# Attention with a bias on one core: a planner's new settings (grouped outputs, 17 listed VectorE slots, throttled first loads, later copies of V)

## The chip, the cores and the metric

The kernel runs on one core of a Trainium2 chip. The metric is the device time of one execution in microseconds, the median of several runs. Lower is better.

## The reference

For 4 x 8 heads of 1024 rows and 64 columns, in float32:

```python
scores = q @ k.transpose(0, 1, 3, 2) / np.sqrt(64) + bias        # bias: 1024 x 1024, the same for all heads
scores_max = np.max(scores, axis=-1, keepdims=True)
attn = np.exp(scores - scores_max) / (np.sum(np.exp(scores - scores_max), axis=-1, keepdims=True) + 1e-8)
out = attn @ v
```

## The kernel before

**Slots.** A head's 1024 query rows are cut into 8 chunks of 128. One chunk of one head is a *slot*; there are 256. The 32 heads form 16 pairs, the pairs two groups of 7 and 9 (`GROUPS`). A slot needs the 128 x 1024 scores (transposed, keys on partitions) in PSUM, their exponential in bfloat16 in SBUF, and the product with V.

**Three places.** PSUM holds three score tiles, `places[0..2]` (the profile calls them `pl`). Place x takes only slots with first index x. Bias is not added for each head: it is written once into a place by a matmul (L241, 8 matmuls), and each later slot of the same chunk adds to what stands there the new head's scores minus the old head's (`fill`, L244, 8 matmuls of 128 columns; the operands `ko`, `qo` and the negated copies `ke`, `qe` of two heads are stacked for that). 17 slots start a chunk and need the bias matmuls: 0 to 2, 42 to 44, 56, 70 to 72, 166 to 168, 186 and 202 to 204. A place can be filled anew only after its reader has finished.

**Exponentials.** ScalarE takes most slots with one ACTIVATE (`exp`, L258, 128 x 1024) into one of `NE` = 13 tiles `E`. Some slots of place 2 go to VectorE instead, in six steps (`d_steps`): `dy` (L275) reads the place and frees it, then `df`, `dt`, `df`, `dt`, `de` (L280 to L295) work in SBUF. The place is free after `dy`; the rest may be spread out.

**Outputs.** `av` (L312) multiplies a slot's E tile with V: 8 matmuls of 65 columns, V's 65th column being ones, so that the row sum comes along. Seven or six outputs share a PSUM bank `po`; `evac` then divides on VectorE (`rs` L320, `ob` L322) and the stores go out by SP's queue, the last ones by ScalarE's. A bank with a single output uses the one tile `olast`; `ob` has two buffers.

**Loads.** GpSimd's queue loads q, k, v and bias and casts them to bfloat16 (L138 to L165). Raw q and k are transposed by TensorE into `px` (L187, L191), copied out by VectorE (`ko` L199, `qo` L201), and doubled or negated (L210 to L218) or moved by SP's queue (L538). V is copied on VectorE from its landing tile (two buffers) into a ring `vall` (L492). The first pass is the 28 loads that carry pairs 0 to 6 and all bias; pairs 7 to 15 (`EARLY` = 7 onward) follow. For these later loads `issue` puts a one-element GpSimd copy into `tick` (L467) ahead of a load, which waits until the load two before has landed (`LATE` = 2). The first pass has no such wait; its loads wait only for free buffers.

**The order is planned while the program is built.** Each engine's queue is in order. A loop at the end of the kernel keeps a clock for each engine (`t_pe`, `t_act`, `t_dve`, `t_pool`), estimated costs (`FILL`, `AV`, `EXP`, ...) and landing times (`raw_at`, `vland_at`, `bias_at`), and always emits the step that could start first by these clocks. `pe_cands` offers TensorE fills, output matmuls and transposes, `pe_pick` chooses; `dve_pick` chooses for VectorE among copies, evacuations and the steps of VectorE slots. A slot goes to VectorE if `may_d` allows it and the estimated VectorE backlog is below `ROOM`. `DUE` gives the slot by which a later pair's transposes shall be done. Where a clock is wrong, the order stays as planned and the engine waits on the chip.

In this order TensorE's outputs are planned slot by slot, because `round_of` has one value for each slot:

```python
group = [s for s in avq[:1] if round_of[s] == round_of[avq[0]]]
```

Of the kernel before, what the change touches and what calls it, by code (L numbers as in the profile page):

```python
# [16 lines left out]
def kernel(  # L17
# [33 lines left out]
    NE = 13  # L51
# [37 lines left out]
    slots = []  # L89
    round_of = []  # L90
    first_pair, split_pair, group_of = set(), set(), {}
    pr0 = 0
    for g, n in enumerate(GROUPS):
        heads = list(range(2 * pr0, 2 * (pr0 + n)))
        rounds = []
        a = (len(heads) * 2 // 3 + 1) // 2 * 2
        tail = [(2, c, h, h == heads[a]) for c in (3, 4) for h in heads[a:]]
        assert len(tail) <= a
        middle = [[(0, 3, h, h == heads[0]), (1, 4, h, h == heads[0])] + tail[i:i + 1] for i, h in enumerate(heads[:a])]
        ends = [[[(x, c + x, h, h == heads[0] and (go or g == 0)) for x in range(3)] for h in heads]  # L100
                for go, c in enumerate((5, 0) if g % 2 else (0, 5))]
        rounds = ends[0] + middle + ends[1]
        first_pair.add(pr0)
        group_of[pr0] = g
        split_pair.add(heads[a] // 2)
        for r in rounds:
            round_of += [len(slots)] * len(r)
            slots += r
        pr0 += n
# [13 lines left out]


    dslots = set()
    may_d = [x[0] == 2 and 36 < s < NS - 18 and not any(y[3] for y in slots[s:s + 4]) for s, x in enumerate(slots)]

# [207 lines left out]
    with tc.manual_schedule():  # L335
# [15 lines left out]
        nc.gpsimd.memset(qs[D:, :, :], 0.0)  # L351
        for c in (1, 2):
            load_b(c)
        load_k(1)
        load_q(1, slice(0, C0))
        load_v(0)
        load_k(2)
        load_q(2, slice(0, NCH))
        for i in range(10):
# [33 lines left out]

        FILL, BIAS, AV = 452, 500, 264
        L_PE, L_ACT, L_DVE = 205, 210, 140
# [3 lines left out]
        bias_at = {0: T0, 1: T0, 2: 9600}  # L399
        raw_at = {(1, 1, 0): 10800, (1, 0, 0): 11500, (2, 1, 0): 14300, (2, 0, 0): 16000}  # L400
        v_at, vland_at = {}, {0: 13000}
        t_dma = 15900
        DUE = (64, 82, 94, 106, 117, 126, 134, 142, 150)
        t_pe, t_act, t_dve, t_pool = 9300.0, 9900.0, 9600.0, 9000
# [27 lines left out]
        TR, SWITCH = 56, 190  # L432
        LATE, QCOST = 2, 4400
        flight = []
        LAG, AVG = 7, 247
# [4 lines left out]
        ROOM = 5000  # L440
        MARGIN = 0
        WINDOW = 4
# [13 lines left out]
        def freed(pr, t):  # L456

            free_lands.add(pr)
            while loads and loads[0] - LANDS in free_lands:
                load(loads.pop(0), t)  # L460

        def issue(at, cost, depth, load, pr, *a):

            nonlocal t_dma
            if 0 < depth <= len(flight):
                what, t = flight[-depth]
                nc.gpsimd.tensor_copy(tick[:], what)  # L467
                at = max(at, t + 100)
            at = pool(at, 750)
            t_dma = max(t_dma + cost, at + 2200 + cost)  # L470
            flight.append((load(pr, *a), t_dma + 200))
            return t_dma + 200
# [17 lines left out]
        def move_v(pr):  # L490
            def run(t2):
                nc.vector.tensor_copy(vall[:, 2 * pr % VR:2 * pr % VR + 2, :, :D], lands[pr, "v"][:])  # L492
                v_at[pr] = t2 + 480 + L_DVE
                next_v(v_at[pr])
            dve_q.append((vland_at[pr], 0.3, 480, run))


        def early(kind, pr):
            if kind == "k":
                raw_at[pr, 1, 0] = issue(0, 1600, 0, load_k, pr) + SLACK  # L500
            elif kind == "q":
                cs = slice(0 if pr >= SPLIT else C0, NCH)
                raw_at[pr, 0, cs.start] = issue(0, 1600 if pr >= SPLIT else 1100, 0, load_q, pr, cs) + SLACK
            elif kind == "v":
                vland_at[pr] = issue(0, 1600, 0, load_v, pr)
                move_v(pr)
            else:
                bias_at[pr] = issue(0, 1600, 0, load_b, pr)

# [65 lines left out]
        def pe_cands():  # L575

            out = []
            for x in range(3):
# [4 lines left out]
                if r is not None and (before[s] is None or before[s] in used):  # L583
                    cost = FILL + BIAS * bool(slots[s][3] and s > 1)

                    def do(t, s=s, x=x, cost=cost):
# [4 lines left out]
                        next_fill = min([y[0] for y in queue.values() if y], default=NS)  # L591
                        if may_d[s] and backlog(t) < ROOM and len(open_d) < 3:
                            dslots.add(s)
# [7 lines left out]
            todo = []  # L601
            if avq:
                group = [s for s in avq[:1] if round_of[s] == round_of[avq[0]]]
                have = [s for s in group if s in e_at]
                lag = len([s for s in avq[:NE] if s in e_at])
                if len(have) < len(group):
                    group = have if lag >= LAG and have[:1] == avq[:1] else []
                if avq[0] >= NS - 3:
                    group = [s for s in avq[:1] if s in e_at]
                if group and all(slots[s][2] // 2 in v_at for s in group):  # L610
                    todo.append((max(max(e_at[s], v_at[slots[s][2] // 2]) for s in group), group))
            if dav:
                todo.append((dav[0][0], [dav[0][1]]))
            if todo:
                r, group = min(todo)
                b = len(closed)
                if b_tag:
                    tag = b_tag[0]
                    group = group[:7 - len(bank[b][1])]
# [3 lines left out]
                cost = AVG * len(group) if len(group) > 1 else AV  # L623
                if r < 1e11:
                    def do(t, group=group, b=b, tag=tag, cost=cost):
# [10 lines left out]
                        n = len(bank[b][1])  # L636
                        if n == 7 or n == 6 and not (dav and dav[0][0] < t + cost + 600) or len(av_done) in (NS - 1, NS):
                            closed.append(b)
                            b_tag.clear()
                            close(b, tag, t + cost + L_PE)  # L640
                    out.append((max(t_pe, r), cost, do, 1, 0))
            if pieces:
# [4 lines left out]
                if ((pr, which, c0) in raw_at and next_fill >= need - AHEAD and (ring < 0 or last_slot[ring] < next_fill)  # L647
                        and (lag < 4 or need - next_fill < 8)):
# [3 lines left out]
                    urgent = need - next_fill < 12  # L652
                    if r < 1e11:
                        def do(t, pr=pr, which=which, c0=c0, n=n, tag=tag, cost=cost):
# [15 lines left out]
                            dve_q.append((t + cost + L_PE, 0 if urgent else 2, 60 * n + (180 if which else 300), run))  # L670
                        out.append((max(t_pe, r), cost, do, 2 if next_fill < need - 9 else 0.5, 0))
            return out
# [19 lines left out]
        chains, d_wait, open_d = [], [], set()  # L692

        def backlog(t):
            x = max(0, t_dve - t) + sum(y[2] for y in dve_q if y[0] < t + 3000 and y[1] < 3)
            return x + sum(sum(y[0] for y in c) for c in chains) / 2 + sum(sum(y[0] for y in c[1:]) for r, s, c in d_wait) / 2

# [32 lines left out]
        def pe_pick():  # L730
# [5 lines left out]
            if others and NE <= next_act < len(acts) and acts[next_act - NE] not in av_done:  # L736

                return min(others, key=lambda x: (x[3] != 1, x[0]))
            now = [x for x in fills if x[0] <= t_pe]
            if now:  # L740


                short = len([s for s in avq[:NE] if s in e_at]) > NE - 3
                due = [x for x in others if x[3] in ((0.5, 1) if short else (0.5,)) and x[0] <= t_pe]
                if due and act_free() - FILL - L_PE - MARGIN > t_pe + due[0][1]:
# [10 lines left out]
        def dve_pick():  # L756
            can = [x for x in dve_q if x[1] < 4 or len(dav) < 2]
            if not can:
# [4 lines left out]
            if best[1] >= 3:  # L763
                soon = [x for x in dve_q if x[1] < 3 and x[0] < start + 350]
                if soon:
# [3 lines left out]
        move_v(0)  # L769
        for x in ("k3", "q3", "v1", "k4", "q4", "v2", "k5", "q5", "v3", "k6", "q6", "v4", "v5", "b3", "q0", "q1", "b4", "v6", "b5", "b6", "b7"):  # L770
            early(x[0], int(x[1]))
        while next_fill < NS or next_act < len(acts) or avq or dav or dve_q or sp_q:
            c = []
            if next_act < len(acts):
# [21 lines left out]
            if who == 0:  # L796
# [3 lines left out]
                next_act += 1  # L800
                used[s] = e_at[s] = t_act + L_ACT
            elif who == 1:
                dve_q.remove(d)
# [39 lines left out]
```

## Time and profile before

| | |
|---|---|
| median of 3 runs | 233.25 us (232.87 to 233.69) |
| the profiled execution | 235.16 us, span 233.4 us from its first to its last instruction |
| granted TensorE clock, mean | 0.997 |
| ACTIVATE rows of exponentials | 237 (235 whole, 2 halves of slot 0) |
| VectorE slots | 20 |
| matmuls and transposes | 4671 rows |
| DMA | 29.75 MB, mean 127 GB/s |

The profile gives each engine's busy time, a timeline with starts and lengths, the waits (who waited for whom), the chain of work that ended last, and the DMA issues with their time to landing. Rows of ScalarE and TensorE overlap their neighbours, so the distance between starts, not the length of a row, is an instruction's cost in a full stretch. In the timeline, neighbouring rows of the same kind are merged, with a count behind "x", and the idle time before a row stands in brackets with what ended it.

### The profile page before, as it was taken

To read this page: it belongs to the slowest core of one execution; us is meant where nothing else is said; L and a number is where in the kernel's file an instruction comes from. 1 tells how busy PE (TensorE), PEld (TensorE's weight loads), DVE (VectorE), ACT (ScalarE), POOL (GpSimd) and SP (SyncE) were. 2 spreads that over 40 slices of the span, in tenths; PEclk is the share of its full clock that TensorE was granted. 3 is DMA by queue.
4 is the path that set the end of the run, shared out by engine and by line. 5 is a ranking of instruction groups with operands and counts; after the bars stand their busy time and mean duration, and the time that the engine had idled before them with its cause. 6 is when DMAs were issued, how large, how long until landed. Compare 5 with 4: busy or idle time off the path is not lost. (4 is left out here: it accounts for less than half of the span.)

```text
span 233.4 us, 10703 instructions
## 1 busy us (share of the span) xinstructions
PE 222.3 (95%) x4671; PEld 209.3 (90%) x4671; DVE 201.5 (86%) x296; ACT 221.1 (95%) x241; POOL 63.4 (27%) x99
## 2 busy tenths in 40 slices
PE   7989999899999999999999997999999999999992
PEld 2869999798999999999999997999999999999982
DVE  2576677599999998999999869999998999999972
ACT  3799999988999999999999998999999999999993
POOL 8943135055446555245352310000000000000000
PEclk9999999999999999999999999999999999999998
DMA  6999979959999899999999992111111111221212
GB/s 206 206 205 215 224 166 158 229 121 150 120 191 137 131 159 183 204 196 157 197 163 201 204 194 68 44 42 39 44 37 42 45 42 42 65 59 42 66 48 56
DMA packets 55646, 29.75 MB, mean 127 GB/s; under 512 B 31472, under 2 KB 51952, under 8 KB 55600
## 3 DMA queue, kind: packets, MB, share of 16 engines
q0 software_dynamic: 30336, 14.06, 48.7%
q1 hardware_dynamic: 24832, 14.40, 22.6%
q8 instruction: 36, 0.59, 1.1%
q10 hardware_dynamic: 432, 0.62, 0.8%
q14 instruction: 10, 0.08, 0.1%
HBM read 29.36 MB, written 8.39 MB: 162 GB/s over the span
## 5 line engine op out<-in xcount | busy, mean ns | idle before, releaser
L258 ACT ACTIVATE E<-pl 128x1024 bf16<-128x1024 f32 (+1 forms) x237 | 218.0, 1089 | 4.3 <-PE pl L244 3.9
L312 PE MATMUL po<-vall,E 128*128 128x65 bf16 x1888 | 93.6, 194 | 0.9 <-ACT E L258 0.9
L312 PEld LDWEIGHTS <-E 128*128 128x128 bf16 x1888 | 78.1, 98 | 1.9 <-ACT E L258 1.2
L244 PE MATMUL pl<-qo,ko 128*128 128x128 bf16 x1024 | 77.3, 219 | 1.7 <-DVE dy L275 1.1
L244 PEld LDWEIGHTS <-ko 128*128 128x128 bf16 x1160 | 69.2, 98 | 4.5 <-issue 1.5
L244 PE MATMUL pl<-qe,ke 128*128 128x128 bf16 x888 | 66.8, 219 | 1.9 <-DVE qe L212 0.5
L244 PEld LDWEIGHTS <-ke 128*128 128x128 bf16 x888 | 53.2, 98 | 5.0 <-issue 1.3
L275 DVE TENSOR_SCALAR dy<-pl 128x1024 int32<-128x1024 f32 x20 | 24.4, 1220 | 2.1 <-PE pl L244 1.4
L322 DVE TENSOR_TENSOR ob<-po,rs 128x448 f32<-128x448 f32 (+2 forms) x39 | 23.2, 594 | 1.9 <-DVE rs L320 0.5
L295 DVE SCALAR_TENSOR_TENSOR de<-dy,dt 128x1024 uint16<-128x1024 int32 x20 | 24.4, 1218 | 0.0
L290 DVE SCALAR_TENSOR_TENSOR dt<-df,dt 128x1024 f32<-128x1024 f32 x20 | 24.4, 1218 | 0.0
L284 DVE SCALAR_TENSOR_TENSOR dt<-df 128x1024 f32<-128x1024 f32 x20 | 24.3, 1217 | 0.0
L287 DVE SCALAR_TENSOR_TENSOR df<-dt,df 128x1024 f32<-128x1024 f32 x20 | 24.3, 1216 | 0.0
L199 DVE COPY ko<-px 128x1024 bf16<-128x1024 bf16 (+1 forms) x16 | 10.7, 671 | 6.9 <-PE px L191 6.3
L165 POOL DMA_DIRECT2D v<-in_v_dram x16 | 11.4, 712 | 18.3 <-DVE vall L492 16.0
L138 POOL DMA_DIRECT2D q<-in_q_dram x18 | 16.0, 890 | 1.3 <-DMA out_dram<-ob 0.5
L201 DVE TENSOR_SCALAR qo<-px,sgn 128x1024 bf16<-128x1024 bf16 (+2 forms) x18 | 12.4, 688 | 4.4 <-PE px L191 3.6
L280 DVE TENSOR_SCALAR df<-dy 128x1024 f32<-128x1024 uint16 x20 | 13.8, 690 | 0.0
L241 PE MATMUL pl<-ident,braw 128*128 128x128 bf16 x136 | 11.5, 228 | 0.1
L145 POOL DMA_DIRECT2D k<-in_k_dram x15 | 11.0, 734 | 2.2 <-PE pl L244 1.0
L320 DVE RECIPROCAL rs<-po 128x7 f32<-128x7 f32 (+3 forms) x40 | 7.8, 195 | 4.4 <-PE po L312 4.0
L467 POOL COPY tick<-q 1x1 bf16<-1x1 bf16 x9 | 3.8, 421 | 24.7 <-DMA q<-in_q_dram 24.7
(54 smaller groups left out, 129.5 us busy)
## 6 DMA issues: line engine op xcount, KB each, us to landing
v<-in_v_dram POOLq DMA_DIRECT2D x16, 256.0 KB, 6.1
k<-in_k_dram POOLq DMA_DIRECT2D x15, 256.0 KB, 5.6
out_dram<-ob SPq DMA_DIRECT2D x32, 96.0 KB, 3.6
out_dram<-ob SPq DMA_DIRECT2D x45, 64.0 KB, 3.2
ke<-ko SPq DMA_DIRECT2D x22, 128.0 KB, 4.9
q<-in_q_dram POOLq DMA_DIRECT2D x18, 128.0 KB, 4.8
qe<-q SPq DMA_DIRECT2D x17, 128.0 KB, 4.9
out_dram<-ob SPq DMA_DIRECT2D x67, 32.0 KB, 1.8
```

The costliest lines, as they stand in the source:

```text
L138: nc.gpsimd.dma_start(out=t[:, :, y, :], in_=(qf, kf)[x][pr][:, y].rearrange("p (c d) -> p c d", d=D))
L201: nc.vector.tensor_scalar(t["qo"][:, cs, :], px[:], sgn[:], None, op0=ALU.mult)
L244: nc.tensor.matmul(to, kk[:, kc, :], qq[:, c, :], start=False, stop=True, skip_group_check=True)
L258: nc.scalar.activation(e[:, i:i + n].rearrange("p b x -> p (b x)"), places[slots[s][0]][:, i:i + n].rearrange("p b x -> p (b x)"), ACTF.Ex ...
L275: w.tensor_scalar(t["y"][:], places[slots[s][0]].rearrange("p b x -> p (b x)"), scale * LOG2E * 65536.0, 127.0 * 65536.0, op0=ALU.mult, op ...
L280: w.tensor_scalar(t["f"][:], t["lo"], G / 65536.0, None, op0=ALU.mult)
L284: w.scalar_tensor_tensor(t["t"][:], t["f"][:], -G, t["f"][:], op0=ALU.add, op1=ALU.mult)
L287: w.scalar_tensor_tensor(t["f"][:], t["t"][:], Q, t["f"][:], op0=ALU.mult, op1=ALU.add)
L290: w.scalar_tensor_tensor(t["t"][:], t["f"][:], V, t["t"][:], op0=ALU.add, op1=ALU.mult)
L295: w.scalar_tensor_tensor(etile[s].bitcast(U16).rearrange("p c q -> p (c q)"), t["y"][:], 1.0 / 512.0, t["t"][:], op0=ALU.mult, op1=ALU.add)
L312: nc.tensor.matmul(po[:, j + i, :], etile[s][:, kc, :], vall[:, slots[s][2] % VR, kc, :], start=j + i + kc == 0, stop=kc == NCH - 1, skip_ ...
L322: nc.vector.tensor_tensor(ob[:, :n, :], po[:, :n, :D], rs[:, :n, :].to_broadcast([P, n, D]), op=ALU.mult)
```

## The change

- **Outputs in groups.** `pe_cands` may offer one, two or three output products together, if they follow each other in the queue and belong to the same head; `av` then interleaves their matmuls over the eight blocks of keys. A group is offered if its last exponential is planned to be ready within `WAIT`; its planned costs are 264, 504 and 741 ns. Larger groups rank ahead of smaller ones, and outputs of VectorE slots ahead of both.
- **VectorE slots from a list.** `PLAN` names 17 slots; `may_d`, `ROOM` and `backlog` go.
- **First loads three in flight.** The 21 loads after the first seven are no longer emitted ahead of the loop, but in it, each behind a copy into `tick` that waits for the load three before (`FIRST` = 3). Their order changes a little: v5 and v6 come later, behind b3, the rest of q0 and q1, and b4. Loads of pairs 7 to 15 start when this list is empty. The planned time of a tick copy, 180 ns, is now counted, and a load's planned DMA time is 1420 instead of 1600 ns.
- **Copies of V placed later.** For pairs from 7 on the planner places the copy 2500 ns after the landing that it expects.
- **Margins.** `DUE`, `MARGIN` (0 to 50), the planned landings of the first loads, and several thresholds of `pe_pick`, `pe_cands` and `dve_pick`.

The diff, cut to its core:

```diff
-    may_d = [x[0] == 2 and 36 < s < NS - 18 and not any(y[3] for y in slots[s:s + 4]) for s, x in enumerate(slots)]
+    PLAN = (50, 59, 62, 87, 93, 123, 132, 147, 162, 171, 180, 192, 195, 210, 216, 231, 246)
...
+        flight = [(load_b(1), 7700), (load_b(2), 9000), (load_k(1), 10400), (load_q(1, slice(0, C0)), 11000),
+                  (load_v(0), 12400), (load_k(2), 13800), (load_q(2, slice(0, NCH)), 15800)]
...
-        FILL, BIAS, AV = 452, 500, 264
+        FILL, BIAS, AV = 452, 500, (0, 264, 504, 741)
...
-        DUE = (64, 82, 94, 106, 117, 126, 134, 142, 150)
+        DUE = (34, 108, 102, 116, 123, 136, 128, 98, 110)
...
-            while loads and loads[0] - LANDS in free_lands:
+            while loads and not early_loads and loads[0] - LANDS in free_lands:
...
                 nc.gpsimd.tensor_copy(tick[:], what)
-                at = max(at, t + 100)
+                at = pool(max(at, t + 100), 180)
...
-            dve_q.append((vland_at[pr], 0.3, 480, run))
+            dve_q.append((vland_at[pr] + 2500 * (pr >= EARLY), 0.3, 480, run))
+        def early_at():
+            kind, pr = early_loads[0][0], int(early_loads[0][1])
+            if kind == "v" and pr > 1 and pr - 2 not in v_at or kind in "kq" and pr > LANDS and pr - LANDS not in free_lands:
+                return None
+            return max(t_pool, flight[-FIRST][1] + 100)
...
-                raw_at[pr, 1, 0] = issue(0, 1600, 0, load_k, pr) + SLACK
+                raw_at[pr, 1, 0] = issue(0, 1420, FIRST, load_k, pr) + SLACK
...
-                        if may_d[s] and backlog(t) < ROOM and len(open_d) < 3:
+                        if s in PLAN and len(open_d) < 3:
...
+            for n in range(1, 3 + 1):
+                group = avq[:n]
+                if len(group) < n or group[-1] not in e_at or slots[group[0]][2] // 2 not in v_at or n > 1 and (
+                        slots[group[-1]][2] != slots[group[0]][2] or group[-1] >= NS - 3):
+                    break
+                r = max(v_at[slots[group[0]][2] // 2], *[e_at[s] for s in group])
+                if n == 1 or r <= max(t_pe, todo[0][0]) + WAIT:
+                    todo.append((r, AV[n], group))
...
-                        if n == 7 or n == 6 and not (dav and dav[0][0] < t + cost + 600) or len(av_done) in (NS - 1, NS):
+                        if n == 7 or n == 6 and not (dav and dav[0][0] < t + cost + 2000) or len(av_done) in (NS - 1, NS):
...
-                short = len([s for s in avq[:NE] if s in e_at]) > NE - 3
-                due = [x for x in others if x[3] in ((0.5, 1) if short else (0.5,)) and x[0] <= t_pe]
+                short = len([s for s in avq[:NE] if s in e_at]) > NE - 2
+                due = [x for x in others if x[3] < (1.1 if short else 0.6) and x[0] <= t_pe]
...
-                soon = [x for x in dve_q if x[1] < 3 and x[0] < start + 350]
+                soon = [x for x in dve_q if x[1] < 3 and x[0] < start + 600]
...
-        for x in ("k3", "q3", "v1", "k4", "q4", "v2", "k5", "q5", "v3", "k6", "q6", "v4", "v5", "b3", "q0", "q1", "b4", "v6", "b5", "b6", "b7"):
-            early(x[0], int(x[1]))
+        early_loads = ["k3", "q3", "v1", "k4", "q4", "v2", "k5", "q5", "v3", "k6", "q6", "v4", "b3", "q0", "q1", "b4", "v5", "b5", "v6", "b6", "b7"]
...
+            if early_loads and early_at() is not None:
+                c.append((early_at(), 4))
```

More of the change, by code (lines that the diff above doesn't have):

```diff
@@ L106 @@
         for r in rounds:
-            round_of += [len(slots)] * len(r)
             slots += r
@@ L351 @@
         nc.gpsimd.memset(qs[D:, :, :], 0.0)
[L352 to L358, printed above, removed]
+        flight = [(load_b(1), 7700), (load_b(2), 9000), (load_k(1), 10400), (load_q(1, slice(0, C0)), 11000),
+                  (load_v(0), 12400), (load_k(2), 13800), (load_q(2, slice(0, NCH)), 15800)]
         for i in range(10):
@@ L399 @@
         bias_at = {0: T0, 1: T0, 2: 9600}
-        raw_at = {(1, 1, 0): 10800, (1, 0, 0): 11500, (2, 1, 0): 14300, (2, 0, 0): 16000}
+        raw_at = {(1, 1, 0): 10500, (1, 0, 0): 11100, (2, 1, 0): 14000, (2, 0, 0): 16200}
         v_at, vland_at = {}, {0: 13000}
-        t_dma = 15900
-        DUE = (64, 82, 94, 106, 117, 126, 134, 142, 150)
+        t_dma = 15200
+        DUE = (34, 108, 102, 116, 123, 136, 128, 98, 110)
         t_pe, t_act, t_dve, t_pool = 9300.0, 9900.0, 9600.0, 9000
@@ L432 @@
         TR, SWITCH = 56, 190
-        LATE, QCOST = 2, 4400
-        flight = []
-        LAG, AVG = 7, 247
+        FIRST, LATE, QCOST = 3, 2, 4400
+        WAIT = 200
         free_lands, loads, loads_v = set(), list(range(EARLY, NP)), []
@@ L439 @@
         DEP = 115
-        ROOM = 5000
-        MARGIN = 0
+        MARGIN = 50
         WINDOW = 4
@@ L456, in freed @@
         def freed(pr, t):
-            free_lands.add(pr)
-            while loads and loads[0] - LANDS in free_lands:
+            free_lands.update([pr] * (pr is not None))
+            while loads and not early_loads and loads[0] - LANDS in free_lands:
                 load(loads.pop(0), t)
@@ L494, in run @@
                 next_v(v_at[pr])
-            dve_q.append((vland_at[pr], 0.3, 480, run))
+            dve_q.append((vland_at[pr] + 2500 * (pr >= EARLY), 0.3, 480, run))
[4 more added lines that the diff above has]
+            return max(t_pool, flight[-FIRST][1] + 100)
         def early(kind, pr):
             if kind == "k":
-                raw_at[pr, 1, 0] = issue(0, 1600, 0, load_k, pr) + SLACK
+                raw_at[pr, 1, 0] = issue(0, 1420, FIRST, load_k, pr) + SLACK
             elif kind == "q":
                 cs = slice(0 if pr >= SPLIT else C0, NCH)
-                raw_at[pr, 0, cs.start] = issue(0, 1600 if pr >= SPLIT else 1100, 0, load_q, pr, cs) + SLACK
+                raw_at[pr, 0, cs.start] = issue(0, 1420 if pr >= SPLIT else 1000, FIRST, load_q, pr, cs) + SLACK
             elif kind == "v":
-                vland_at[pr] = issue(0, 1600, 0, load_v, pr)
+                vland_at[pr] = issue(0, 1420, FIRST, load_v, pr)
                 move_v(pr)
             else:
-                bias_at[pr] = issue(0, 1600, 0, load_b, pr)
+                bias_at[pr] = issue(0, 1420, FIRST, load_b, pr)
         def doubles(pr, which, c0, n, t2, urgent):
@@ L601, in pe_cands @@
             todo = []
[L602 to L611, printed above, removed]
+            for n in range(1, 3 + 1):
[6 more added lines that the diff above has]
+                    todo.append((r, AV[n], group))
             if dav:
-                todo.append((dav[0][0], [dav[0][1]]))
-            if todo:
-                r, group = min(todo)
+                todo.append((dav[0][0], AV[1], [dav[0][1]]))
+            for r, cost, group in todo:
                 b = len(closed)
@@ L618, in pe_cands @@
                     tag = b_tag[0]
-                    group = group[:7 - len(bank[b][1])]
+                    if len(group) + len(bank[b][1]) > 7:
+                        continue
                 else:
@@ L622, in pe_cands @@
                     r = max(r, f)
-                cost = AVG * len(group) if len(group) > 1 else AV
                 if r < 1e11:
@@ L640, in do @@
                             close(b, tag, t + cost + L_PE)
-                    out.append((max(t_pe, r), cost, do, 1, 0))
+                    out.append((max(t_pe, r), cost, do, 0.75 if group[0] in dslots else 1.1 - 0.1 * len(group), 0))
             if pieces:
@@ L647, in pe_cands @@
                 if ((pr, which, c0) in raw_at and next_fill >= need - AHEAD and (ring < 0 or last_slot[ring] < next_fill)
-                        and (lag < 4 or need - next_fill < 8)):
+                        and (lag < 7 or need - next_fill < 6)):
                     f, tag = min((x_free[y], y) for y in x_free)
@@ L651, in pe_cands @@
                     cost = n * TR + SWITCH * (pr < EARLY or which not in BESIDE)
-                    urgent = need - next_fill < 12
+                    urgent = need - next_fill < 16
                     if r < 1e11:
@@ L670, in do @@
                             dve_q.append((t + cost + L_PE, 0 if urgent else 2, 60 * n + (180 if which else 300), run))
-                        out.append((max(t_pe, r), cost, do, 2 if next_fill < need - 9 else 0.5, 0))
+                        out.append((max(t_pe, r), cost, do, 2 if next_fill < need - 7 else 0.5, 0))
             return out
@@ L692 @@
         chains, d_wait, open_d = [], [], set()
-        def backlog(t):
-            x = max(0, t_dve - t) + sum(y[2] for y in dve_q if y[0] < t + 3000 and y[1] < 3)
-            return x + sum(sum(y[0] for y in c) for c in chains) / 2 + sum(sum(y[0] for y in c[1:]) for r, s, c in d_wait) / 2
         def start_d(s):
@@ L736, in pe_pick @@
             if others and NE <= next_act < len(acts) and acts[next_act - NE] not in av_done:
-                return min(others, key=lambda x: (x[3] != 1, x[0]))
+                return min(others, key=lambda x: (not 0.7 < x[3] < 1.1, x[0]))
             now = [x for x in fills if x[0] <= t_pe]
             if now:
-                short = len([s for s in avq[:NE] if s in e_at]) > NE - 3
-                due = [x for x in others if x[3] in ((0.5, 1) if short else (0.5,)) and x[0] <= t_pe]
+                short = len([s for s in avq[:NE] if s in e_at]) > NE - 2
+                due = [x for x in others if x[3] < (1.1 if short else 0.6) and x[0] <= t_pe]
                 if due and act_free() - FILL - L_PE - MARGIN > t_pe + due[0][1]:
@@ L756, in dve_pick @@
         def dve_pick():
-            can = [x for x in dve_q if x[1] < 4 or len(dav) < 2]
+            can = [x for x in dve_q if x[1] < 4 or len(dav) < 3]
             if not can:
@@ L801 @@
                 used[s] = e_at[s] = t_act + L_ACT
+            elif who == 4:
+                x = early_loads.pop(0)
+                early(x[0], int(x[1]))
+                freed(None, t)
             elif who == 1:
```

1 line of the change is left out of this document (removed).

## The prediction

> **What bounds the kernel now.** I read the busy times of the page, then ScalarE's timeline, then the waits and the timelines around its gaps, last the loads and the end. A gain or loss below 0.3% (0.7 us) I count as no change; a measurement of this kernel cannot tell less.
>
> From the page:
>
> ```profile
> PE 222.3 (95%) x4671; PEld 209.3 (90%) x4671; DVE 201.5 (86%) x296; ACT 221.1 (95%) x241; POOL 63.4 (27%) x99
> ```
>
> TensorE and ScalarE look equally full, so I ask which of them sets the pace. ScalarE's timeline (start, length, rows merged; idle before):
>
> ```profile
> 9.05 7.93 ACT L258 ACTIVATE E<-pl 128x512 bf16<-128x512 f32 x9 [0.47 <-PE pl L244]
> 17.19 30.08 ACT L258 ACTIVATE E<-pl 128x1024 bf16<-128x1024 f32 x32 [0.21 <-PE pl L244]
> ...
> 55.28 17.52 ACT L258 ACTIVATE E<-pl 128x1024 bf16<-128x1024 f32 x19 [0.59 <-PE pl L244]
> 73.14 69.23 ACT L258 ACTIVATE E<-pl 128x1024 bf16<-128x1024 f32 x75 [0.34 <-PE pl L244]
> 143.24 86.31 ACT L258 ACTIVATE E<-pl 128x1024 bf16<-128x1024 f32 x94 [0.87 <-PE pl L244]
> ```
>
> and two rows of narrower views, a stretch near the end and the last exponential:
>
> ```profile
> 217.40 11.23 ACT L258 ACTIVATE E<-pl 128x1024 bf16<-128x1024 f32 x12
> 228.25 1.31 ACT E L258
> ```
>
> From 217.40 to the last start at 228.25 lie 12 steps: 0.904 us each, though a single row lasts longer (1.02 us alone; rows overlap). That is ScalarE's own pace. Against it: 143.24 to 228.25 holds 93 steps, 85.01 - 93 x 0.904 = 0.94 us lost. 55.28 to 143.24 holds 94: 2.98 lost. 17.19 to 55.28 holds 39 (32 and seven in rows left out here): 2.83 lost. 9.05 to 17.19 (a half of 0.495, eight whole): 0.41 lost. So ScalarE sets the end; all it can win is these 7.16 us, and each exponential more costs 0.904. TensorE has room: a slot is 445 ns of scores and 260 of output matmuls (starts in its timeline), 705 against 904; it costs only where it is late.
>
> Where the 7.16 lies, by starts of exponentials: 1.03 at 46.26 to 50.00, where TensorE does this:
>
> ```profile
> 46.30 0.69 PE L241 MATMUL pl<-ident,braw 128*128 128x128 bf16 x8
> 46.82 0.61 PE L244 MATMUL pl<-qz,ko 128*128 128x128 bf16 x8
> 47.27 0.42 PE L312 MATMUL po<-vall,E 128*128 128x65 bf16 x8
> 47.53 0.69 PE L241 MATMUL pl<-ident,braw 128*128 128x128 bf16 x8
> ```
>
> bias, scores, outputs: 47.53 - 46.30 = 1.23 us per slot, three times. The same at 71.6 (bias slots 70 to 72, after four output groups in a row): 0.65. At 141.3 another 1.03, whose cause stands in VectorE's timeline:
>
> ```profile
> 138.33 0.43 DVE L492 COPY vall<-v 128x1024 bf16<-128x1024 bf16 x1 [1.86 <-DMA v<-in_v_dram]
> 138.68 1.22 DVE L295 SCALAR_TENSOR_TENSOR de<-dy,dt 128x1024 uint16<-128x1024 int32 x1
> 139.81 0.74 DVE L201 TENSOR_SCALAR qo<-px,sgn 128x1024 bf16<-128x1024 bf16 x1
> ...
> 141.32 1.22 DVE L275 TENSOR_SCALAR dy<-pl 128x1024 int32<-128x1024 f32 x1
> ```
>
> A copy of V, placed too early, blocks VectorE 1.86 us for its load; the step that frees place 2 (dy) starts late, and the waits name it: TensorE waits 1.1 us for dy, ScalarE then 0.9. Further: 0.39 at 15.9 and 0.54 at 42 to 44 (transposes wait in TensorE's queue for the loads of q2 and of the rest of q0), 0.25 at 38.2 (a transpose), 0.74 at 53.6 (VectorE slots 47 and 50, dy late). The remaining 2.53 are 20 VectorE slots at about 0.1 each (the last stretch: nine of them, 0.94) and 0.31 and 0.29 at 110.6 and 120.9, a VectorE slot beside a transpose.
>
> **The change, part by part.** *17 VectorE slots instead of 20.* The orders of both programs show 17 dy instructions against 20. Three exponentials return to ScalarE: +3 x 0.904 = **+2.71 us** on the path. VectorE is relieved of 3 x (5 x 1.22 + 0.69) = 20.4 us, beside the path; it goes from 86% to about 77%, so fewer dy come late. The new slots lie 3 to 36 apart; 59 and 62, 192 and 195 still follow each other on place 2. With an exponential as 0.904, 0.24 from its end to the fill, 0.445 fill and 0.26 to the next exponential (rows around 43 and 49.7 us), two remaining places turn in 0.945, so some 0.1 per slot stays. I leave the whole 2.53 in, lower bound 1.36 (17 at 0.08, no collisions), upper 5 (all 17 at 0.3, as at 110.6).
>
> *Groups for one head.* In the new order 114 output groups are single, 35 pairs, 24 triples, and the three bias slots at 42 to 44 stand as bias, scores, bias, scores, bias, scores, outputs in threes behind. Without outputs between, a bias slot takes 0.52 + 0.445 = 0.97 us; three places give TensorE up to 0.86 us of lead, and three times 0.06 over 0.904 uses little of it. So the 1.03 goes, and by the same sum over slots 68 to 73 (five fills, two of them ahead on place 2) the 0.65: **-1.68**. A triple is 0.78 us in a row and delays what is queued behind it on TensorE, scores above all, but the lead covers that; without it, each would cost up to 0.3. Whether interleaved matmuls are cheaper than 260 ns no row shows; sixteen in sequence took 521, twice 260. Within 10% either way on 142 outputs that is 3.7 us of TensorE, covered by 0.2 us of slack per slot: 0, bounds -0.2 and +0.2.
>
> *V copied 2.5 us later.* The 1.86 us wait is covered: **-1.03**. Who waits for V: outputs only, with 13 tiles E between, 11 us.
>
> *Loads three in flight, and their order.* The rest of q0 and q1 now comes before v5 and v6, and q2's transposes stand one fill later: **-0.39 and -0.54**. New is a GpSimd copy (tick) ahead of each of 21 loads; queued behind it on GpSimd are all later loads. A load's latency, and a tick's length:
>
> ```profile
> v<-in_v_dram POOLq DMA_DIRECT2D x1, 256.0 KB, 4.0
> ...
> v<-in_v_dram POOLq DMA_DIRECT2D x1, 256.0 KB, 5.0
> ...
> L467 POOL COPY tick<-k x9: 177/518/803, 54.4 to 120.2; 1x1 bf16<-1x1 bf16 x9
> ```
>
> 4.0 us is a load on an empty queue (issued at 32.77), 5.0 one at 124.9 beside another. I take 4.2 for evenly spaced loads, being nearest to the empty queue, plus 0.5: three loads per 4.7, 1.57 each, against 1.47 in the flood of before (issue plus time to landing: k3 at 16.9, q6 at 31.6, ten loads). k3 may start once v0 has landed (12.3) and lands at 17.4, one load behind q2 (15.9); 13 loads on, the rest of q0 lands at 37.8. Its transposes stand behind fill 34, at about 38.3, and can wait until 39.2 before ScalarE starves. So 0, with a bound from 5.0: rival one.
>
> *Slots 47/50 and the transpose at 38.2:* the first VectorE slot is now 50, **-0.74 and -0.25**.
>
> *The end.* Before, the last two banks hold two and one output, in two tiles; after, one and one, and both go through olast, of which there is one. The new order makes the second multiply wait for the first store:
>
> ```profile
> 229.68 0.38 ACTq L688 DMA_DIRECT2D out_dram<-ob  x1
> 230.28 0.23 DVE L322 TENSOR_TENSOR olast<-po,rs 128x64 f32<-128x64 f32 x1
> 230.53 0.34 ACTq L688 DMA_DIRECT2D out_dram<-olast  x1
> ```
>
> The first store is issued behind the last exponential as now, at 229.63, and lands 1.7 us on (the issue rows of ACT); the multiply then starts at 231.33 instead of 230.28: **+1.05**, nothing hides it (0.8 if the store lands in 1.45, 1.4 if in 2.05). By the Trainium skill, DMA: Bandwidth & Descriptors, "Anatomy of one DMA — SWDGE (gpsimd) path", a transfer costs some 2.0 us fixed, mostly the receipt of the write; an estimate from it is 2.1 us here and +1.4, but that section is of the GpSimd path, and the row of 1.7 decides.
>
> Sum: 2.71 + 1.05 - 1.68 - 1.03 - 0.93 - 0.99 = -0.87 us. The profiled execution took 235.16 (span 233.4, 1.8 around it), 1.9 above the median 233.25; the sum, made on the span, gives 234.3 for it and 232.4 on the median.
>
> **Rivals.** *One, slower: the loads starve.* With 5.0 us latency at three in flight and 0.5 for the tick, a load takes 1.83 us, q0 lands at 41.2, TensorE's queue stands 2.0 us behind its transposes: 234.4. It decides from 1.68 us per load (39.2). For: 5.0 is measured with two in flight; q0 took 8.0 us before. Against: 4.0 on the empty queue, and at 40 us few stores run. The Trainium skill, SBUF — State Buffer, "SBUF: two separate sides", says that GpSimd and a VectorE instruction in a two-port mode exclude each other for the whole instruction, descriptors included; by it a tick may wait out a copy of 0.69 us, an estimate of 1.8 us per load and 1.6 us lost. The ticks' spread, 177 to 803 ns, agrees that they wait for something. Chance 0.2.
>
> *Two, no change: the bubbles do not shrink.* Denser transposes (pairs 8 to 15 between slots 94 and 146) meet VectorE slots 123, 132 and 147, and seven middle slots cost 0.3 instead of 0.1, +1.4 less what the relieved VectorE gives back, 0.6: 233.2. Chance 0.25.
>
> *Three, faster still:* of the 2.53 only 1.36 stays: 231.2. Chance 0.15. That the list of slots is cut short, since a slot is dropped when three are open, the order excludes: all 17 are there.
>
> **Numbers.** Forecast (231.6 to 232.9) 0.35, rivals 0.2, 0.25, 0.15; 0.05 for a mishap beyond. Faster than 232.55 is most of the forecast and rival three: 0.48. Within 0.7 us: rival two and the rest of the forecast: 0.27. Slower: 0.25. The range takes in rival three and rival one: 231.2 to 234.8.
>
> **Right or wrong.** 240 exponentials; from 44 to 52 us and 69 to 74 an unbroken run; no gap at 138 to 143; the second olast over 1 us behind its reciprocal; a start gap total near 2.5 us. Wrong would be: waits of px for qrest, k or q from 30 to 60 us, or gaps of 0.3 at most VectorE slots.

## The result and the profile after

The changed kernel takes 242.62 us (median of 6 runs, 240.14 to 245.43), the kernel before 233.47 (6 runs). The ratio is 1.034, 95% interval 1.030 to 1.038: slower. Ratios, here and below, leave out every run more than 1.5% above the fastest of its kernel; medians take all runs. The forecast was 232.4. The profiled execution took 240.41 us, span 238.5, on the low side of its median.

The page's busy times:

```profile
PE 222.6 (93%) x4671; PEld 208.7 (87%) x4671; DVE 184.8 (77%) x282; ACT 223.8 (94%) x244; POOL 65.0 (27%) x120
```

VectorE is relieved by 16.7 us (201.5 to 184.8; 20.4 was counted, and two output banks more take some of it back). ScalarE has the three exponentials more. Where they start, from ScalarE's timeline:

```profile
8.95 14.35 ACT L255 ACTIVATE E<-pl 128x512 bf16<-128x512 f32 x16 [0.47 <-PE pl L241]
23.86 1.94 ACT L255 ACTIVATE E<-pl 128x1024 bf16<-128x1024 f32 x2 [0.56 <-PE pl L241]
25.99 5.81 ACT L255 ACTIVATE E<-pl 128x1024 bf16<-128x1024 f32 x6 [0.19 <-PE pl L241]
32.00 9.77 ACT L255 ACTIVATE E<-pl 128x1024 bf16<-128x1024 f32 x10 [0.20 <-PE pl L241]
43.15 1.02 ACT L255 ACTIVATE E<-pl 128x1024 bf16<-128x1024 f32 x1 [1.39 <-PE pl L241]
44.64 5.64 ACT L255 ACTIVATE E<-pl 128x1024 bf16<-128x1024 f32 x6 [0.47 <-PE pl L241]
51.97 181.83 ACT L255 ACTIVATE E<-pl 128x1024 bf16<-128x1024 f32 x198 [1.69 <-PE pl L241]
```

From 51.97 on, 198 exponentials run without a gap that ends the row: to the last start at 232.65 they lose 180.68 - 197 x 0.904 = 2.59 us. From 8.95 to 51.97 they lose 43.02 - (0.495 + 40 x 0.904) = 6.36, of which 5.4 at the six breaks between these rows. The kernel before lost 2.49 from 9.05 to 50.00, by the same sum. Against the profiled execution of before the span grows by 5.1 us: 2.71 for three exponentials, 6.36 + 2.59 - 7.16 = 1.79 of losses, 0.70 behind the last start, 0.10 less ahead of the first.

What the gaps wait for, from the waits between 18 and 54 us (waiter, releaser: us in total, times, longest):

```profile
DVE vall L482 <- DMA v<-in_v_dram: 15.7, 6, 3.7
PE px L188 <- DVE ko L196: 3.5, 4, 1.7
PE po L309 <- DVE qo L198: 1.7, 1, 1.7
```

In the kernel before, the first of these came to 0.9 us here. One of the six in the timeline of all engines:

```profile
39.59 0.61 PE L241 MATMUL pl<-qo,ko 128*128 128x128 bf16 x8
39.74 0.43 DVE L482 COPY vall<-v 128x1024 bf16<-128x1024 bf16 x1 [2.92 <-DMA v<-in_v_dram]
...
41.14 0.67 DVE L196 COPY ko<-px 128x1024 bf16<-128x1024 bf16 x1
...
41.86 0.64 PE L188 MATMUL px<-ident,q 128*64 128x128 bf16 x16 [1.66 <-DVE ko L196]
```

VectorE stands 2.92 us at a copy of V whose load has not landed. Behind it in the same queue are the doublings of the previous q and then ko, whose px is full; TensorE's next transposes want a free px and wait 1.66 us, with the scores behind them; then ScalarE starves, 1.39 us ahead of 43.15. The chain of work that ended last goes back through loads in this stretch:

```profile
17.44 5.34 DMA k<-in_k_dram
...
23.35 7.14 DMA k<-in_k_dram
...
31.07 4.54 DMA k<-in_k_dram
...
36.20 6.54 DMA braw<-in_bias_dram
...
44.34 5.23 DMA v<-in_v_dram
```

Five loads, one after the other, each let out by a tick that saw the earlier one land: 28.8 of the 32.1 us from 17.44 to 49.57.

Two things came as forecast. The bias slots now follow at 0.95 us:

```profile
51.71 0.67 PE L238 MATMUL pl<-ident,braw 128*128 128x128 bf16 x8
52.22 0.61 PE L241 MATMUL pl<-qz,ko 128*128 128x128 bf16 x8
52.67 0.66 PE L238 MATMUL pl<-ident,braw 128*128 128x128 bf16 x8
```

and the end waits for the store of the first olast by just the 1.05 us counted:

```profile
233.65 0.22 DVE L319 TENSOR_TENSOR olast<-po,rs 128x64 f32<-128x64 f32 x1
...
234.33 0.17 DVE L317 RECIPROCAL rs<-po 128x1 f32<-128x1 f32 x1 [0.45 <-PE po L309]
235.54 0.22 DVE L319 TENSOR_TENSOR olast<-po,rs 128x64 f32<-128x64 f32 x1 [1.05 <-DMA out_dram<-olast]
```

### The profile page after: what moved, and what is told of

It is laid out like the page before. It is cut to its first block, busy times and chain, and to the rows that moved or that the text cites. A ratio compares the mean times of both kernels' runs of the same rounds, so it can differ in the third digit from the quotient of the medians.

```text
span 238.5 us, 10694 instructions
## 1 busy us (share of the span) xinstructions
PE 222.6 (93%) x4671; PEld 208.7 (87%) x4671; DVE 184.8 (77%) x282; ACT 223.8 (94%) x244; POOL 65.0 (27%) x120
## 4 chain that ended last, share of the span: by engine, by line
PE 47%; ACT 20%; DMA 16%; issue 11%; POOL 4%; DVE 1%; POOLq 0%; ACTq 0%; DVEq 0%
PE pl L241 28%; ACT E L255 20%; PE po L309 14%; DMA k<-in_k_dram 7%; DMA q<-in_q_dram 4%; DMA braw<-in_bias_dram 3%; DMA v<-in_v_dram 2%; PE pl L238 2%; PE px L188 1%; PE px L184 1%; POOL braw L157 1%; DMA out_dram<-olast 1%; POOL k L142 1%; POOL tick L457 1%; POOL v L162 0%
## 5 line engine op out<-in xcount | busy, mean ns | idle before, releaser
L309 PE MATMUL po<-vall,E 128*128 128x65 bf16 x1912 | 84.2, 194 | 2.5 <-DVE qo L198 1.7
L309 PEld LDWEIGHTS <-E 128*128 128x128 bf16 x1912 | 73.4, 98 | 3.0 <-issue 1.9
L319 DVE TENSOR_TENSOR ob<-po,rs 128x384 f32<-128x384 f32 (+1 forms) x40 | 23.2, 581 | 1.6
L272 DVE TENSOR_SCALAR dy<-pl 128x1024 int32<-128x1024 f32 x17 | 20.8, 1223 | 4.3 <-PE pl L241 4.2
L292 DVE SCALAR_TENSOR_TENSOR de<-dy,dt 128x1024 uint16<-128x1024 int32 x17 | 20.7, 1219 | 0.1
L284 DVE SCALAR_TENSOR_TENSOR df<-dt,df 128x1024 f32<-128x1024 f32 x17 | 20.7, 1217 | 0.1
L281 DVE SCALAR_TENSOR_TENSOR dt<-df 128x1024 f32<-128x1024 f32 x17 | 20.7, 1217 | 0.1
L287 DVE SCALAR_TENSOR_TENSOR dt<-df,dt 128x1024 f32<-128x1024 f32 x17 | 20.7, 1217 | 0.0
L482 DVE COPY vall<-v 128x1024 bf16<-128x1024 bf16 x16 | 7.4, 466 | 15.7 <-DMA v<-in_v_dram 15.7
L317 DVE RECIPROCAL rs<-po 128x6 f32<-128x6 f32 (+2 forms) x42 | 8.2, 195 | 12.6 <-PE po L309 11.7
```

The source lines that it names most:

```text
L272: w.tensor_scalar(t["y"][:], places[slots[s][0]].rearrange("p b x -> p (b x)"), scale * LOG2E * 65536.0, 127.0 * 65536.0, op0=ALU.mult, op ...
L281: w.scalar_tensor_tensor(t["t"][:], t["f"][:], -G, t["f"][:], op0=ALU.add, op1=ALU.mult)
L284: w.scalar_tensor_tensor(t["f"][:], t["t"][:], Q, t["f"][:], op0=ALU.mult, op1=ALU.add)
L287: w.scalar_tensor_tensor(t["t"][:], t["f"][:], V, t["t"][:], op0=ALU.add, op1=ALU.mult)
L292: w.scalar_tensor_tensor(etile[s].bitcast(U16).rearrange("p c q -> p (c q)"), t["y"][:], 1.0 / 512.0, t["t"][:], op0=ALU.mult, op1=ALU.add)
L309: nc.tensor.matmul(po[:, j + i, :], etile[s][:, kc, :], vall[:, slots[s][2] % VR, kc, :], start=j + i + kc == 0, stop=kc == NCH - 1, skip_ ...
```

## The experiments

Each ratio is against runs of the kernel before on the same chip. Its median there was 233.8 us for the throttle taken away, the ticks without a wait, the throttle in the kernel before and the two last tiles; 234.1 for six in flight, the groups alone and the 19 slots; 234.7 for the order of the first loads; 234.6 for the other four. "Loss" is what ScalarE loses over its own pace from the second start to the last, as worked out above: 7.16 before, 8.95 after.

**The throttle, taken away with all other orders kept.**

```diff
-                nc.gpsimd.tensor_copy(tick[:], what)
+                if depth != FIRST:
+                    nc.gpsimd.tensor_copy(tick[:], what)
```

> The changed kernel without the 21 tick copies of the first pass; the orders on TensorE, VectorE, ScalarE and SP stay the same, the loads run freely again. Theory (waiting for a landing before each load makes V late, its copy blocks VectorE, then ko, px and TensorE wait): nearly all of the 6.2 us that ScalarE loses between 22 and 52 us goes, span near 232.7, time 232.5 to 233.5, VectorE waits under 3 us for V. Rival (the new order itself, its groups, slots and places of copies, loses the time): stays above 238.

Measured: 235.81 us, ratio 1.0058 (1.0028 to 1.0088). That is 6.6 us below the changed kernel by the ratios (1.0342 - 1.0058, of 233.8) and 6.8 by the medians; the loss is 4.34, so that the two traces show 4.6 of it. TensorE, VectorE and ScalarE run the same instructions in the same order, so the tick copies with their waits alone cost this. ScalarE and VectorE (18 to 54 us) of this run:

```profile
9.27 21.68 ACT L255 ACTIVATE E<-pl 128x512 bf16<-128x512 f32 x24 [0.47 <-PE pl L241]
31.50 5.61 ACT L255 ACTIVATE E<-pl 128x1024 bf16<-128x1024 f32 x6 [0.55 <-PE pl L241]
37.56 191.94 ACT L255 ACTIVATE E<-pl 128x1024 bf16<-128x1024 f32 x209 [0.46 <-PE pl L241]
```

```profile
DVE vall L483 <- DMA v<-in_v_dram: 1.2, 1, 1.2
```

The waits for V are nearly gone (15.7 to 1.2 us), and most of the gaps. The time expected was 2 to 3 us too low: what is left is slower than the kernel before.

**The tick copies kept, their wait taken away.**

```diff
+                nc.gpsimd.tensor_copy(tick[:], flight[0][0] if depth == FIRST else what)
```

> The changed kernel with all 21 tick copies of the first pass, but each reads an element of the first bias load, which has long landed, so that it waits for nothing. Theory (the wait for the landing costs): within 0.7 us of the kernel without ticks. Rival (the copies themselves cost, by GpSimd's time of 0.2 to 0.4 us each and by shutting out, or being shut out by, VectorE): 21 x 0.4 = 8 us of GpSimd's queue, loads a third later, time 236 to 240.

Measured: 236.04 us, ratio 1.0074 (1.0043 to 1.0105), 0.2 us over no copies at all. The copies cost nothing that shows; the wait for a landing does. By the Trainium skill, SBUF — State Buffer, "SBUF: two separate sides", I had let the copies be held up by VectorE, an estimate of 1.8 us per load. In this run the 21 copies took 0.18 to 0.27 us each, and the first pass ran as well as without them, so that rule decided nothing here. Later in the same run, where VectorE has steps of its own slots to do, the trace agrees with the rule, since this tick copy ends only when the step does (72.31 against 72.28 us):

```profile
71.07 1.21 DVE L284 SCALAR_TENSOR_TENSOR df<-dt,df 128x1024 f32<-128x1024 f32 x1
71.23 1.08 POOL L457 COPY tick<-k 1x1 bf16<-1x1 bf16 x1
```

**The wait made six deep instead of three, the same orders.**

```diff
+                nc.gpsimd.tensor_copy(tick[:], flight[-6][0] if depth == FIRST else what)
```

> The changed kernel with its orders on the other engines, its 21 tick copies now waiting for the load six before instead of three. Theory (three in flight cannot hide a load's 4.4 to 7 us from issue to landing; the loss is a matter of depth): with six, 7 us over 6 are 1.2 us per load, below the 1.5 of free loads, so 235.5 to 236.5, as without any wait. Rival (any wait of GpSimd's in-order queue for a landing costs, since a k behind it waits too): 238 or more.

Measured: 236.29 us, ratio 1.0093 (1.0059 to 1.0127), near the free loads and 6 us below three deep; loss 3.77. The ticks still wait here (3.4 us for q and 1.1 for V between 8 and 45 us), but k3 lands at 17.0 and the rest of q0 at 35.8 (issued at 27.61, 8.2 us to landing): 1.45 us per load, against 2.05 with three. So it is the depth, not that there is a wait.

**The throttle put into the kernel before.** Its orders stay; each of its 21 loads gets a tick copy from the load three before.

> The kernel before with the one edit that each of the 21 loads of its first pass stands behind a tick copy that waits for the load three before; the orders on the other engines are those of before. Theory: V and k come late as in the changed kernel, VectorE and TensorE wait, 238 to 243 us. Rival (only the new order cannot stand later loads): under 235.

Measured: 242.05 us, median of 4 (239.67 to 245.39); ratio 1.023 (1.015 to 1.031), from two of them. The old order suffers too, near the 2.8% of the new one; the rival, under 235, is out. The size rests on two runs.

**V copied later in the first pass too, throttle kept.**

```diff
-            dve_q.append((vland_at[pr] + 2500 * (pr >= EARLY), 0.3, 480, run))
+            dve_q.append((vland_at[pr] + 2500, 0.3, 480, run))
```

> The changed kernel, throttle kept, with the 2500 ns margin for copies of V in the first pass too (the planner then orders anew). Theory (late V lands while its copy stands at the head of VectorE's queue, and ko and px wait behind it): VectorE's waits for V fall from 15.7 us to under 5, ScalarE's loss between 20 and 54 us from 6.2 to 2 to 3, time 237 to 240. Rival (V is late for the outputs themselves, wherever its copy stands; k and q are late as well): 241 or more.

Measured: 246.94 us, ratio 1.052 (1.046 to 1.057): a miss, and on the rival's side. The planner ordered everything anew here, so more than the copies of V moved. VectorE's waits for V did fall, to 7.4 us, but now TensorE itself meets late loads (its waits, 18 to 70 us):

```profile
PE po L309 <- DVE vall L482: 2.3, 1, 2.3
PE px L188 <- DMA k<-in_k_dram: 2.2, 1, 2.2
```

So the copy of V was the first victim of late loads, not the fault: planned later, it leaves TensorE to meet a late V and a late k. Part of the longer time has another cause, told in the last section.

**Two tiles for the last two banks**, on top of the free loads.

```diff
-    olast = consts.tile([P, 1, D], F32)
+    olast = [consts.tile([P, 1, D], F32, name=f"olast{x}") for x in range(2)]
...
+        ob = olast[b % 2] if n == 1 else op.tile([P, 7, D], F32, name="ob")
```

> As the kernel without the ticks of the first pass, and the last two banks of one output each have a tile of their own instead of sharing olast. Theory of the end (the second multiply waits for the first store): 1.0 us less than without this edit, 231.4 to 232.5, the second multiply at once behind its reciprocal. Rival (the last store lands when it lands, as stores of one queue follow each other): within 0.3 us.

Measured: 235.06 us, ratio 1.0046 (1.0016 to 1.0077): 0.75 below the free loads by the medians and 0.3 by the ratios, less than the 1.0 expected. The second multiply follows its reciprocal:

```profile
229.72 0.17 DVE L317 RECIPROCAL rs<-po 128x1 f32<-128x1 f32 x1 [0.46 <-PE po L309]
229.92 0.22 DVE L319 TENSOR_TENSOR olast<-po,rs 128x64 f32<-128x64 f32 x1
```

From the last start of an exponential to the end it is 5.1 us, against 5.9 with one tile: some 0.7 of the 1.05 comes back.

**Three VectorE slots fewer, in the kernel before.**

```diff
-                        if may_d[s] and backlog(t) < ROOM and len(open_d) < 3:
+                        if may_d[s] and backlog(t) < ROOM and len(open_d) < 3 and len(dslots) < 17:
```

> The kernel before with its last three VectorE slots (216, 225, 234) left to ScalarE, 17 in all. Term of the forecast: 3 x 0.904 more, 3 x 0.1 of bubbles less, +2.4 us (ratio 1.009 to 1.011). Rival (VectorE's relief gives it back): under +1 us.

Measured: 236.80 us, ratio 1.0105 (1.0066 to 1.0144), +2.5 us by the ratio and +2.2 by the medians: the term of the forecast is right. The run tells more. Its order up to slot 207 is that of before, yet at 125 to 145 us VectorE waits for V only

```profile
DVE vall L492 <- DMA v<-in_v_dram: 1.1, 2, 0.7
```

and ScalarE's gap of 1.03 us at 141 us is not there:

```profile
17.40 29.61 ACT L258 ACTIVATE E<-pl 128x1024 bf16<-128x1024 f32 x32 [0.20 <-PE pl L244]
47.25 1.02 ACT L258 ACTIVATE E<-pl 128x1024 bf16<-128x1024 f32 x1 [0.24 <-PE pl L244]
48.48 1.02 ACT L258 ACTIVATE E<-pl 128x1024 bf16<-128x1024 f32 x1 [0.20 <-PE pl L244]
49.72 22.28 ACT L258 ACTIVATE E<-pl 128x1024 bf16<-128x1024 f32 x24 [0.21 <-PE pl L244]
72.33 158.22 ACT L258 ACTIVATE E<-pl 128x1024 bf16<-128x1024 f32 x172 [0.33 <-PE pl L244]
```

The loss is 4.87 in all. The profiled execution of before, 1.9 us above its median, had losses that others don't have.

**Later copies of V alone, in the kernel before.** The edit is the changed kernel's (2500 ns from pair 7 on).

> The kernel before with the one edit that copies of V of pairs from 7 on are planned 2500 ns later. Forecast's term: the gap of 1.03 us at 141.3 us goes, 1.0 us faster (ratio 0.995 to 0.997). Rival (VectorE is 86% full, so that the copy meets another step and another gap opens): within 0.3%.

Measured: 234.26 us, ratio 0.9986 (0.9958 to 1.0015): no change that shows; loss 5.10. The rival holds, but, by the run with 17 slots, for another cause than it gave: there is mostly nothing to win at 141 us.

**And with it the changed order of the first loads, freely emitted** (b3, the rest of q0 and q1 and b4 ahead of v5, q2 expected at 16400).

> The kernel before with two parts of the change that need no extra waits: later copies of V from pair 7 on, and the first pass in the changed order (b3, the rest of q0 and q1 and b4 ahead of v5), with q2 expected 0.4 us later. Theory (what ScalarE loses at 16 and 42 us is loads met too early): 0.5 to 1.0 us faster than the kernel before (ratio 0.996 to 0.998). Rival (the planner answers with other slots and other bubbles, as it did for the V edit alone): within 0.3%.

Measured: 234.74 us, ratio 0.9998 (0.9974 to 1.0023). No change; the rival again. In its profile, of an execution 1 us above the median, the rest of q0 and q1 has landed by 37.3 us, and yet ScalarE loses 0.57 at 40.1 and 0.79 at 44.5 us.

**Grouped outputs alone, in the kernel before.** The offer of one to three outputs, with costs and ranks, as in the diff.

> The kernel before with the grouped outputs alone (the offer of one to three outputs of a head, their planned costs and ranks); the planner then also picks its 20 VectorE slots anew, and its last two banks share olast. Term of the forecast: the losses of about 1.0 at 46 to 50 us and 0.6 at 71 us go, 1.7 us gained, less 1.05 for the end: 0.3 to 0.8 us faster (ratio 0.996 to 0.999). Rival (TensorE is full where bias comes, groups only move the wait): slower by 0.5 to 1.5 us, mostly from the end.

Measured: 235.85 us, ratio 1.0091 (1.0059 to 1.0123): slower where a gain was expected, a miss. The planner answered with other VectorE slots (75 and 78 became 75 and 81, and so on) and lost 6.82 us, 0.9 of it at 43 us, where TensorE waits 0.87 for the rest of q; its end has the olast wait (the waits of VectorE):

```profile
DVE olast L322 <- DMA out_dram<-olast: 1.2, 1, 1.2
```

So this run doesn't isolate the groups; it shows that in a planned order one part brings others along.

**Free loads that the planner knows of, two last tiles, the rest as changed.** Loads as in the kernel before, with its planned costs.

> The changed kernel with the loads of the first pass emitted freely as in the kernel before, in its order and with its planned costs, so that the planner knows it, and two tiles for the last two banks; groups, 17 listed slots, later copies of V and margins stay. Theory (the order made for throttled loads puts V copies and transposes wrongly once loads are free, and this is the 1.8 us lost between 29 and 42 us): 1.0 to 1.6 us below the free loads with two last tiles, 233.4 to 234.2. Rival (TensorE is full in this stretch whatever the plan): 235.

Measured: 235.62 us, ratio 1.0059 (1.0026 to 1.0092). That is no lower than the free loads with two last tiles (1.0046): the theory missed, and the rival's 235 came. The loss is 3.80, with six in flight (3.77) the smallest of all; ScalarE's timeline has just two long rows, from 9.27 to 47.7 us and from 47.97 on. So the order itself became good, by more than a microsecond against the old order (4.87 with 17 slots, 5.10 with V later), and that is less than the three exponentials, 2.71.

**The same with VectorE slots by the old rule (19).**

> Free loads known to the planner, grouped outputs, later copies of V, two tiles for the last two banks, and VectorE slots by the rule of the kernel before (19 come out) instead of the list of 17. Theory (each slot on VectorE is worth 0.8 us): 1.6 us below the same kernel with 17 slots, so about level with or 0.5 us below the kernel before (ratio 0.995 to 1.000). Rival (more slots meet more bubbles in a fuller VectorE): no gain over 17, ratio 1.005.

Measured: 236.48 us, ratio 1.0101 (1.0059 to 1.0143): above both the theory and the rival. The two exponentials saved came back as stalls: loss 5.93, with 0.8 at 41 us, three gaps of 0.33 to 0.35 at the bias slots and 0.5 at 59, 72 and 182. At the bias slots TensorE does what it did before, bias, scores, one output, 1.24 us per slot (bias at 46.31, 47.55 and 48.78), though groups are offered: the offer alone does not remove these gaps. None of the versions beats the kernel before.

## Why the prediction was wrong

**The step that failed** is "Loads three in flight", where the forecast took 4.2 us for a load's latency, 0.5 for the tick, 1.57 us per load, and 0 for the cost. Issue plus time to landing in the profile after: k3 at 16.9, the rest of q0 at 43.5 (38.37 + 5.1), 13 loads in 26.6 us, 2.05 each. The latencies of these loads were 4.4 to 7.1 us, 5.45 on average, and from a landing to the issue that waited for it passed some 0.6: the latency was the mis-sized term. A load late by itself delayed the issue of all behind it in GpSimd's queue. Rival one had the mechanism and the price per load nearly (1.83), and the point from which it decides, 1.68, was passed; but I gave it 0.2. It also named the wrong first victim. I counted when TensorE would meet q0's transposes at 39 us, and wrote that only outputs wait for V. On VectorE everything queued behind the copy of V waits, so ScalarE had already lost 0.8 us at 23 us. Together with its follow-ups the step costs 6.6 us (6.8 by the medians) where 0 stood.

**The gains taken from one execution** were the second fault. I noted that the profiled execution was 1.9 us over the median and still subtracted its gaps as if they were the kernel's. The profiles with 17 slots and with V later have the same order in the first 70 us, and the one with 17 slots at 141 us too. There the 1.03 at 141 us and the 0.54 at 42 to 44 are missing, and the 0.74 at 53.6 is 0.23. The rest recurs: 0.40 and 0.48 at 16 us for the 0.39, 0.26 for the 0.25, 1.6 at the bias slots for the 1.68. So some 2.1 of the 4.63 were not there to be won. With them left out the forecast's own sum is +1.2 instead of -0.87.

That is near the run on free loads, where the changed kernel stands 1.4 us (by the ratio) to 2.0 us (by the medians) above before: this fault alone turns the sign of the forecast, and the failed step adds 6.6 us. The slots cost 2.2 to 2.5 and the end up to 0.75, so all gains come to about 1 to 1.9 us. By the rows at 51.7 us and the two long rows of the replanned kernel, most of it is the 1.68 for the bias slots; that is argued and not shown, since no run has the groups' share alone.

**Right were** three exponentials at 0.904 (the kernel before with 17 slots), ScalarE as the bound, the olast wait (1.05 in the trace, 0.3 to 0.75 in the time), and the bubbles: 2.59 us for 198 steps and 17 slots, no 0.3 at each slot, so rival two did not come.

What stays open is the rest of the median: the changed kernel's six runs spread from 240.1 to 245.4, and only a short one has a profile. The last section shows what can lengthen the others.

## What to carry to other kernels

A limit on loads in flight must cover the landing time that is measured under load, here 4.4 to 7.1 us, against some 1.5 us from one load to the next when nothing holds them: at three deep it costs 3%, at six nothing that shows; four and five were not run. Price a late load at the first in-order queue that meets it, and count what stands behind the waiting instruction there. And before subtracting a gap, see whether a second execution has it.

## What the hardware did that I had not expected

In these traces a stall of TensorE of more than 2 us costs more than its own length. In the run with V later everywhere, TensorE was idle 2.29 us ahead of 49.73, and then (busy us of PE, PEld, DVE, ACT and POOL, granted clock, DMA share, GB/s):

```profile
47.00:50.00 3.00, 0.71 (x17) 0.54 (x15) 0.76 (x2) 2.38 (x3) 1.44 (x4) 1.00 1.02 199
50.00:53.00 3.00, 3.00 (x49) 3.00 (x46) 1.22 (x4) 1.15 (x2) 1.20 (x3) 0.67 1.03 144
53.00:56.00 3.00, 3.00 (x48) 3.00 (x47) 0.00 (x0) 2.32 (x3) 0.00 (x0) 0.77 0.67 116
```

```profile
51.72 1.06 PE L241 MATMUL pl<-qz,ko 128*128 128x128 bf16 x8
52.57 1.06 PE L238 MATMUL pl<-ident,braw 128*128 128x128 bf16 x8
```

Eight score matmuls took 0.85 us from start to start instead of 0.445. The means of 0.67 and 0.77 come to half a clock for 3.4 us, and ScalarE lost 0.8 at each of the two bias slots. It is no single case. In the same run TensorE was idle 2.23 us ahead of 60.93, and in the kernel before with the throttle 2.39 us ahead of 59.89; then, in this order:

```profile
62.00:65.00 3.00, 3.00 (x41) 3.00 (x40) 1.77 (x3) 1.10 (x2) 1.05 (x3) 0.56 1.32 126
60.00:63.00 3.00, 3.00 (x47) 3.00 (x46) 3.00 (x4) 1.56 (x2) 2.24 (x4) 0.61 0.85 84
```

Behind the gaps of 1.66 and 1.75 us in the changed kernel, and of 1.78 and 1.73 in the kernel before with the throttle, the granted clock stayed at 1.00. The Trainium skill, TensorE: Matmul & The Clock Gate, "HAM oscillation — how this bites in real kernels", describes such a drop to half speed and asks for no idle gap above 3.4 us; here gaps of 2.23 to 2.39 were each followed by one. The profiled execution of the changed kernel shows no such stretch, but its longest run has a lower mean clock (0.984 at a span of 243.4, 0.996 at 238.5), which would agree. The 0.990 to 0.992 of three others says less, since runs without any such gap have 0.991 too (that with 19 slots); no profile of a long one was taken.
